# Sums of weights formed on GpSimd instead of VectorE in a Strassen-like feed-forward layer

## The chip, the cores and the metric

The kernel runs on one core of one Trainium2 chip. The metric is the device time of one execution in microseconds; the median over the timed runs is compared. The names of engines are those of the profile: PE is TensorE (its matmuls; PEld its weight loads), DVE is VectorE, ACT is ScalarE, POOL is GpSimd, and SP is SyncE, whose queue issues most DMAs.

## The reference, cut to what matters

One inference step of a small backbone: 2 layers, 640 tokens (512 latent and 128 context), model width 1024. Each layer is a half-step feed-forward, a token mixer (a two-dimensional Fourier transform in the first layer, attention in the second), and another half-step feed-forward, so there are four feed-forward stages in all. Each stage computes

```
def _swiglu(h, w1, w2):
    gate, up = jnp.split(h @ w1, 2, axis=-1)
    return (jax.nn.silu(gate) * up) @ w2
```

with a hidden width of 2816, which is 22 tiles of 128 ("f tiles"). Everything is float32. The other inputs are modulation weights (w_mod), which are multiplied with two condition vectors in the background of the other work.

## The kernel before, in words

**Precision.** Each product of float32 matrices is made as three matmuls of rounded parts (`mm3`, lines 228 to 230). For it every operand is split into a rounded part "hi", written by ACT (line 215), and the rest "lo" = operand - hi, written by DVE (line 216). Both the weights and the activations go through this split. Weight tiles are 128 x 1024 (a "unit"); they come by DMA into one of four buffers named raw, and the parts lie in six buffers each, named hi and lo. A unit is asked for three units ahead of its use in the code; the planner of the framework lays out the order on each engine from its own model of durations, so the splits run further ahead, as far as buffers allow.

**Seven products instead of eight.** The tokens are cut into two halves of 320. For the f tiles 4 to 21 (18 of 22 in each stage, 72 in all; `w1_fast`) the product of a 1024 x 256 piece of w1 (gate and up columns) with the two halves is made as a two-by-two block product in seven block products (Winograd's form of Strassen's method). Each block product is 4 x 3 = 12 matmuls of 128 x 320. To this end sums of the blocks are needed:

- Sums of activations, made once per stage (`combine`): b12 - b11 and so on, split into parts and kept in `sums[1]` to `sums[4]`.
- Sums of weights, made once per f tile (`send`, kinds "sums", "all" and "u2"). With `one` the first 512 columns of a raw tile and `two` the second 512: line 179 forms gate1 + up1, line 180 forms up1 + up2 in place, line 181 forms gate1 + (up1 + up2), and line 188 (for the last two f tiles of a stage line 197) forms the fourth one from the third and gate2. Each is one DVE instruction over 128 x 512.

In the code of one f tile (`w1_fast`, `one`, `two`) the order of products is: the first into bank x (kind main), the second into y (kind score), the third into z (main), the fourth into w (main), and then the fifth, sixth and seventh add to x, z and w. Between them small instructions on 128 x 320 read these banks: ACT copies x (line 687) before the fifth product may add to it; DVE forms q (690) from y, a (693) from z before the sixth may add to z, a again (713) from w before the seventh; the rest (698, 701, 702, 719 to 721) forms the hidden values, which are split again and kept for the second weight matrix. The main kind has four banks, the score kind two.

**Stages and slices.** After every fourth fast f tile a slice of the second matrix (w2) follows: 8 row tiles x 2 halves x 4 f tiles x 3 = 192 matmuls. Its results are added up by ACT, which puts the earlier sum into the bank before (line 737) and takes it out after (line 763). In the slices the background jobs run as well (line 421: one DMA of a raw tile of w_mod and two DVE instructions over 128 x 1024), 36, 12, 28, 32, 12 and 8 jobs in the six sub-layers.

**Order.** Each engine works through its own queue in order. A DVE instruction that stands behind a waiting one waits too, and so do those of ACT. POOL has hardly anything to do in the kernel before: a reciprocal root of three columns per normalisation (line 507), a few small differences and memsets in attention (lines 1041 and 1054), and two instructions in the last step (`leave`, lines 585 and 595).

Of the kernel before, what the change touches and what calls it, by code (L numbers as in the profile page):

```python
# [15 lines left out]
ALU = mybir.AluOpType  # L16
# [94 lines left out]
class Kernel:  # L111
# [54 lines left out]
    def send(self, kind, src):  # L166

        nc, two, one = self.nc, slice(512, UNIT), slice(0, 512)
        at = slice(0, UNIT)
        if kind in ("plain", "block", "gate"):
            raw = self.raw_tile(src)
            self.fast["gate"] = raw
        elif kind == "sums":
            up, gate = self.raw_tile(src), self.fast["gate"]
            raw = self.raw.tile([P, UNIT], F32, tag="raw", name=self.name("sums"))
            nc.vector.tensor_tensor(raw[:, one], gate[:, one], up[:, one], op=ALU.add)
            nc.vector.tensor_tensor(up[:, one], up[:, one], up[:, two], op=ALU.add)  # L180
            nc.vector.tensor_tensor(raw[:, two], gate[:, one], up[:, one], op=ALU.add)  # L181
            self.fast["up"], self.fast["sums"] = up, raw
        elif kind in ("up", "u2"):
            raw = self.fast["up"]
            at = at if kind == "up" else two
        else:
            raw, at = self.fast["gate"], two
            nc.vector.scalar_tensor_tensor(out=raw[:, two], in0=self.fast["sums"][:, two], scalar=-1.0,
                                           in1=raw[:, two], op0=ALU.mult, op1=ALU.subtract)
        n = at.stop - at.start  # L190
        if kind == "block":
            hi, lo = (self.ring(F32R)[:, :n] for _ in range(2))
        else:
            hi, lo = (self.wts.tile([P, UNIT], F32R, tag=tag, name=self.name(tag))[:, :n] for tag in ("hi", "lo"))
        self.split(hi, lo, raw[:, at])
        if kind == "u2":
            nc.vector.scalar_tensor_tensor(out=raw[:, two], in0=self.fast["sums"][:, two], scalar=-1.0,
                                           in1=self.fast["gate"][:, two], op0=ALU.mult, op1=ALU.subtract)
            self.mixed.append(raw)
        return hi, lo  # L200

# [400 lines left out]
    def ffn(self, layer, which, base, boundary):  # L602
# [43 lines left out]
        def combine(step):  # L646
# [10 lines left out]
            if step < 2:  # L657
                t = combine.now[k] = [self.temp(("square", "total")[step]).rearrange("p (c t) -> p c t", c=2)
                                      for _ in range(2)]
                steps = ((1, t[0], b12, b11), (2, t[1], b22, t[0]))  # L660
            else:
                t = combine.now[k]
                steps = ((3, t[0], b22, b12), (4, t[1], t[1], b21))
            for i, to, a, b in steps:
                if k == 0:
                    sums[i] = [quad(self.ring(F32R)) for _ in range(2)]
                nc.vector.tensor_tensor(to, a, b, op=ALU.subtract)
                self.split(sums[i][0][:, k : k + 2, :], sums[i][1][:, k : k + 2, :], to)

        high, tt = self.tc.high_priority, nc.vector.tensor_tensor  # L670
# [38 lines left out]
        def one(f, a, unit):  # L709
            w = self.bank()[:, :HALF]  # L710
            product(f, w, unit, 0, lambda k: part(1, k), True)
            with high():
                tt(a, a, w, op=ALU.add)
            return w

        def two(f, a, q, w, unit, at):
            product(f, w, unit, at, lambda k: self.h.chunk(4 + k, 1), False)
            with high():
                nc.vector.scalar_tensor_tensor(out=q, in0=w, scalar=-1.0, in1=q, op0=ALU.mult, op1=ALU.subtract)  # L719
                nc.scalar.activation(q, q, AF.Silu)  # L720
                tt(a, a, q, op=ALU.mult)
                hidden(f, a, 1)
# [708 lines left out]
```

## Time and profile before

| | |
|---|---|
| median of 3 runs | 2283.66 us |
| lowest and highest run | 2283.55 and 2283.94 us |
| span of the profiled execution (first to last instruction) | 2280.3 us |
| busy PE | 2250.1 us, 99% |
| busy DVE | 1732.2 us, 76% |
| busy ACT | 1269.6 us, 56% |
| busy POOL | 43.1 us, 2%, 64 instructions |
| mean granted clock of TensorE | 0.995 |

The time of the profiled execution outside its span isn't listed by itself; the median of the runs lies 3.4 us above the span. Busy times are shares of the span; matmuls overlap in the pipeline (one lasts about 310 ns but the next starts 147 ns after it), so a busy PE is to be checked against the distance of starts. In a row of a group stand the line, the engine, the operation, the tiles written and read with their shapes, the count, the busy time, the mean duration of one in ns, and the idle time of the engine ahead of it with what ended it.

### The profile page before, as it was taken

The page shows a single profiled execution, that of the slowest core. Times are in us where ns is not written, and L with a number is a line of the kernel's source. Part 1 is how long each engine was busy: PE and PEld are TensorE (multiplying, and loading weights), DVE is VectorE, ACT ScalarE, POOL GpSimd, SP SyncE. Part 2 cuts the span into 40 slices and gives each one's busy share as a digit, 9 for nine tenths or more (in the row PEclk, how much of TensorE's full clock was granted, in tenths as well). Part 3 has the DMA queues.
Part 4 walks back from the last instruction along what each step waited for, and adds up shares of the span by engine and source line. Part 5 has one row for each costly group of instructions (what it writes and reads, how often), then busy time and mean ns, then how long its engine had stood idle before and what let it go on. Part 6 is the DMA issues. An engine that isn't in the chain of part 4 may idle for free.

```text
span 2280.3 us, 39327 instructions
## 1 busy us (share of the span) xinstructions
PE 2250.1 (99%) x15680; PEld 2211.6 (97%) x15680; DVE 1732.2 (76%) x3014; ACT 1269.6 (56%) x2460; POOL 43.1 (2%) x64
## 2 busy tenths in 40 slices
PE   7999999999999999999999999999999999999998
PEld 5999999999999999999999999998998999999998
DVE  5889888588788888868878888587667485766674
ACT  4445554565654555556545544567778654545545
POOL 0000000000000000000000000000000000000000
PEclk9999999999999999999999999999999999999999
DMA  8244543434333433443234443324333223322322
GB/s 313 88 138 150 162 133 113 147 97 129 112 112 112 148 121 125 135 157 112 92 123 145 151 130 110 140 92 140 112 108 116 67 74 101 111 93 76 104 92 100
DMA packets 80281, 278.14 MB, mean 122 GB/s; under 512 B 8800, under 2 KB 15200, under 8 KB 79968
## 3 DMA queue, kind: packets, MB, share of 16 engines
q1 hardware_dynamic: 79280, 274.63, 36.4%
q8 instruction: 123, 2.02, 0.3%
q10 hardware_dynamic: 816, 0.98, 0.1%
q14 instruction: 62, 0.51, 0.1%
HBM read 264.04 MB, written 11.53 MB: 121 GB/s over the span
## 4 chain that ended last, share of the span: by engine, by line
PE 95%; DVE 2%; DMA 1%; ACT 1%; issue 0%; DVEq 0%; POOL 0%; SPq 0%
PE main L228 28%; PE main L230 27%; PE main L229 27%; PE score L229 3%; PE score L228 3%; PE score L230 3%; PE sum L1262 1%; PE score L1219 1%; PE sum L512 1%; PE sum L502 1%; DMA first<-in_w_mod_k 1%; PE turn L1246 1%; DVE lo L216 0%; PE main L1246 0%; DVE ring L1065 0%
## 5 line engine op out<-in xcount | busy, mean ns | idle before, releaser
L228 PE MATMUL main<-ring,hi 128*128 128x320 f32 x3872 | 1206.5, 312 | 2.0 <-ACT ring L215 1.6
L229 PE MATMUL main<-ring,hi 128*128 128x320 f32 x3872 | 1198.2, 310 | 1.0 <-DVE ring L216 1.0
L230 PE MATMUL main<-ring,lo 128*128 128x320 f32 x3872 | 1198.4, 310 | 0.0
L228 PEld LDWEIGHTS main<-ring,hi 128*128 128x128 f32 x3872 | 728.0, 188 | 8.4 <-issue 4.1
L229 PEld LDWEIGHTS main<-ring,hi 128*128 128x128 f32 x3872 | 728.3, 188 | 2.1 <-DVE ring L216 1.6
L230 PEld LDWEIGHTS main<-ring,lo 128*128 128x128 f32 x3872 | 728.0, 188 | 0.6 <-issue 0.5
L215 ACT ACTIVATE hi<-raw 128x1024 fp32r<-128x1024 f32 (+1 forms) x366 | 356.0, 974 | 433.7 <-PE main L229 349.2
L216 DVE TENSOR_TENSOR lo<-raw,hi 128x1024 fp32r<-128x1024 f32 (+1 forms) x366 | 409.0, 1118 | 140.8 <-ACT hi L215 139.4
L421 DVE SCALAR_TENSOR_TENSOR junk<-raw,wide 128x1024 bf16<-128x1024 f32 x256 | 312.7, 1222 | 19.7 <-DMA raw<-in_w_mod_t 17.2
L763 ACT ACTIVATE y<-main 128x320 f32<-128x320 f32 x318 | 135.7, 432 | 150.1 <-PE main L230 149.4
L737 ACT ACTIVATE main<-y 128x320 f32<-128x320 f32 x256 | 111.4, 439 | 39.2 <-DVE left L719 27.0
L228 PE MATMUL score<-ring,hi 128*128 128x320 f32 x416 | 128.9, 310 | 0.0
L230 PE MATMUL score<-ring,lo 128*128 128x320 f32 x416 | 128.6, 309 | 0.0
L229 PE MATMUL score<-ring,hi 128*128 128x320 f32 x416 | 128.5, 309 | 0.0
L216 DVE TENSOR_TENSOR lo<-sums,hi 128x1024 fp32r<-128x1024 f32 x72 | 88.0, 1222 | 42.6 <-ACT hi L215 42.6
L457 DVE TENSOR_TENSOR total<-total,square 128x640 f32<-128x640 f32 x71 | 58.4, 824 | 79.9 <-ACT square L456 78.2
L215 ACT ACTIVATE hi<-sums 128x1024 fp32r<-128x1024 f32 x72 | 76.3, 1060 | 33.8 <-DVE sums L181 19.6
L228 PE MATMUL main<-ring,ring 128*128 128x320 f32 x288 | 90.9, 316 | 0.0
L230 PE MATMUL main<-ring,ring 128*128 128x320 f32 x288 | 89.1, 310 | 0.0
L229 PE MATMUL main<-ring,ring 128*128 128x320 f32 x288 | 88.9, 309 | 0.0
L228 PEld LDWEIGHTS score<-ring,hi 128*128 128x128 f32 x416 | 78.1, 188 | 0.0
L229 PEld LDWEIGHTS score<-ring,hi 128*128 128x128 f32 x416 | 78.1, 188 | 0.0
(195 smaller groups left out, 2604.8 us busy)
## 6 DMA issues: line engine op xcount, KB each, us to landing
raw<-in_w SPq DMA_DIRECT2D x264, 512.0 KB, 3.6
raw<-in_w_mod_t SPq DMA_DIRECT2D x128, 512.0 KB, 4.1
raw<-in_qkv SPq DMA_DIRECT2D x26, 512.0 KB, 3.7
first<-in_w_mod_k SPq DMA_DIRECT2D x16, 512.0 KB, 8.9
spill<-ring SPq DMA_DIRECT2D x12, 640.0 KB, 3.8
ring<-spill SPq DMA_DIRECT2D x12, 640.0 KB, 7.0
raw<-in_bias SPq DMA_DIRECT2D x16, 448.0 KB, 3.4
raw<-in_four_in SPq DMA_DIRECT2D x8, 512.0 KB, 5.7
```

What stands on the lines that cost most here:

```text
L215: a = self.nc.scalar.activation(hi, src, AF.Copy)
L216: return a, self.nc.vector.tensor_tensor(lo, src, hi.bitcast(F32), op=ALU.subtract)
L228: mm(out, whi, xhi, start=start, stop=False)
L229: mm(out, whi, xlo, start=False, stop=False)
L230: self.latest = mm(out, wlo, xhi, start=False, stop=stop)
L421: last = self.nc.vector.scalar_tensor_tensor(out=self.junk, in0=raw, scalar=1.0, in1=self.wide[:, cond, :], op0=ALU.mult, op1=ALU.mult, ac ...
L457: nc.vector.tensor_tensor(acc, acc, sq, op=ALU.add)
L502: self.meant = nc.tensor.matmul(ps[:, j : j + 1], part[:, t : t + P], self.mean, start=i == j == 0 or len(acc) == 1, stop=i == len(acc) - ...
L512: self.spread = nc.tensor.matmul(bank[:, t : t + P], col[:, j : j + 1].to_broadcast([P, P]), self.ident, start=True, stop=True)
L737: nc.scalar.activation(ps[:, :HALF], self.y[:, m, lo:hi], AF.Copy)
L763: nc.scalar.activation(self.y[:, m, lo:hi], ps[:, :HALF], AF.Copy)
L1219: nc.tensor.matmul(o, q, k[:, BLOCK_KEYS[b]], start=part == 0, stop=part == 1)
```

## The change

The three sums of kind "sums" and the fourth one of kinds "all" and "u2" go from `nc.vector` to `nc.gpsimd`. The fourth was formed as (-1) x sums - gate2 in one instruction of the kind scalar_tensor_tensor. On GpSimd it is a plain add, sums + gate2, which is the negative of what it was. To keep the result, the activation sum that meets w's products is formed with the opposite sign as well (b11 - b12 instead of b12 - b11, and the next sum adds it instead of subtracting it), so that bank w holds the negative of what it held, and the two DVE instructions that read w (lines 713 and 719 before) subtract in place of adding, and w - q in place of -w - q. The count of instructions is the same: 288 move from DVE to POOL (72 at each of lines 179 to 181, 64 at line 188, 8 at line 197).

```
         elif kind == "sums":
             up, gate = self.raw_tile(src), self.fast["gate"]
             raw = self.raw.tile([P, UNIT], F32, tag="raw", name=self.name("sums"))
-            nc.vector.tensor_tensor(raw[:, one], gate[:, one], up[:, one], op=ALU.add)
-            nc.vector.tensor_tensor(up[:, one], up[:, one], up[:, two], op=ALU.add)
-            nc.vector.tensor_tensor(raw[:, two], gate[:, one], up[:, one], op=ALU.add)
+            nc.gpsimd.tensor_tensor(raw[:, one], gate[:, one], up[:, one], op=ALU.add)
+            nc.gpsimd.tensor_tensor(up[:, one], up[:, one], up[:, two], op=ALU.add)
+            nc.gpsimd.tensor_tensor(raw[:, two], gate[:, one], up[:, one], op=ALU.add)
             self.fast["up"], self.fast["sums"] = up, raw
...
-            nc.vector.scalar_tensor_tensor(out=raw[:, two], in0=self.fast["sums"][:, two], scalar=-1.0,
-                                           in1=raw[:, two], op0=ALU.mult, op1=ALU.subtract)
+            nc.gpsimd.tensor_tensor(raw[:, two], self.fast["sums"][:, two], raw[:, two], op=ALU.add)
...
         if kind == "u2":
-            nc.vector.scalar_tensor_tensor(out=raw[:, two], in0=self.fast["sums"][:, two], scalar=-1.0,
-                                           in1=self.fast["gate"][:, two], op0=ALU.mult, op1=ALU.subtract)
+            nc.gpsimd.tensor_tensor(raw[:, two], self.fast["sums"][:, two], self.fast["gate"][:, two], op=ALU.add)
...
-                steps = ((1, t[0], b12, b11), (2, t[1], b22, t[0]))
+                steps = ((1, t[0], b11, b12, ALU.subtract), (2, t[1], b22, t[0], ALU.add))
...
-                steps = ((3, t[0], b22, b12), (4, t[1], t[1], b21))
-            for i, to, a, b in steps:
+                steps = ((3, t[0], b22, b12, ALU.subtract), (4, t[1], t[1], b21, ALU.subtract))
+            for i, to, a, b, op in steps:
...
-                nc.vector.tensor_tensor(to, a, b, op=ALU.subtract)
+                nc.vector.tensor_tensor(to, a, b, op=op)
...
             with high():
-                tt(a, a, w, op=ALU.add)
+                tt(a, a, w, op=ALU.subtract)
...
-                nc.vector.scalar_tensor_tensor(out=q, in0=w, scalar=-1.0, in1=q, op0=ALU.mult, op1=ALU.subtract)
+                tt(q, w, q, op=ALU.subtract)
```

## The prediction

> **What bounds the kernel now.** I read the page first (busy shares, the strip of slices, the chain that ended last), then busy time by stretch.
>
> ```profile
> span 2280.3 us, 39327 instructions
> PE 2250.1 (99%) x15680; PEld 2211.6 (97%) x15680; DVE 1732.2 (76%) x3014; ACT 1269.6 (56%) x2460; POOL 43.1 (2%) x64
> ...
> PE 95%; DVE 2%; DMA 1%; ACT 1%; issue 0%; DVEq 0%; POOL 0%; SPq 0%
> ```
>
> TensorE holds 95% of the chain. A busy PE need not be at its peak, so I check the rate in a stretch that the change touches. One f tile with seven products runs 7 x 12 matmuls; its second product goes to a bank named score, so the first score matmul marks the tile. The next two fences are the timeline of TensorE, and then the busy time of one whole cycle (four fast f tiles and one slice of the second weight matrix, 77.44 us) in each of the four feed-forward stages.
>
> ```profile
> 212.37 0.31 PE L228 MATMUL score<-ring,hi 128*128 128x320 f32 x1
> ...
> 302.12 0.31 PE L228 MATMUL score<-ring,hi 128*128 128x320 f32 x1
> ...
> 314.44 0.31 PE L228 MATMUL score<-ring,hi 128*128 128x320 f32 x1
> ```
>
> ```profile
> 133.17:210.61 77.44, 77.44 (x531) 77.44 (x530) 68.29 (x111) 40.53 (x72) 0.00 (x0) 1.00 0.44 142
> 717.56:795.00 77.44, 77.44 (x530) 77.44 (x529) 63.96 (x104) 40.71 (x72) 0.00 (x0) 1.00 0.40 130
> 1158.22:1235.66 77.44, 77.44 (x530) 77.44 (x529) 65.85 (x106) 40.59 (x72) 0.00 (x0) 1.00 0.42 136
> 1929.59:2007.03 77.44, 77.44 (x530) 77.44 (x529) 51.95 (x80) 40.85 (x72) 0.00 (x0) 1.00 0.30 96
> ```
>
> After the stretch and its length the columns are the busy time of PE, PEld, DVE, ACT, POOL, then clock and DMA. Tile follows tile after 314.44 - 302.12 = 12.32 us, which is 84 matmuls at 0.1467 us; 528 matmuls (4 x 84 and 192 for the slice) at 0.1467 are 77.45 us, the whole cycle. So PE has no hole in these cycles, at full clock. A product of 12 matmuls is 1.76 us. DVE is the second engine: 68.29 of 77.44 (88%) in the first stage, 83%, 85% and 67% in the others.
>
> **What the change can win at most.** Where sums are formed outside these cycles, PE is short of the stretch by this much:
>
> ```profile
> 399.00:684.00 285.00, 284.89 (x1989) 280.12 (x1988) 219.83 (x366) 165.72 (x319) 9.63 (x8) 1.00 0.35 119
> 969.00:1117.00 148.00, 147.01 (x1006) 145.64 (x1005) 110.89 (x169) 89.74 (x167) 3.78 (x4) 1.00 0.34 119
> 1482.00:1824.00 342.00, 335.70 (x2569) 314.87 (x2567) 240.55 (x614) 250.46 (x622) 18.49 (x37) 0.99 0.34 106
> ```
>
> That is 0.11 and 0.99 us at the two crossings between stages; the 6.30 us of the third stretch lie in attention, which forms no sums. So the relief of DVE is worth at most about 1 us directly.
>
> **Removed from DVE.** The rows by line and form:
>
> ```profile
> L181 DVE TENSOR_TENSOR sums<-raw,raw 128x512 f32<-128x512 f32 x72 | 49.7, 691 | 1.9
> L180 DVE TENSOR_TENSOR raw<-raw 128x512 f32<-128x512 f32 x72 | 49.7, 690 | 1.7
> L179 DVE TENSOR_TENSOR sums<-raw,raw 128x512 f32<-128x512 f32 x72 | 49.4, 686 | 16.3 <-DMA raw<-in_w 15.7 <-DVE left L713 0.4
> L188 DVE SCALAR_TENSOR_TENSOR raw<-sums,raw 128x512 f32<-128x512 f32 x64 | 44.1, 689 | 0.9
> L197 DVE SCALAR_TENSOR_TENSOR raw<-sums,raw 128x512 f32<-128x512 f32 x8 | 5.5, 689 | 0.1
> ```
>
> 49.7 + 49.7 + 49.4 + 44.1 + 5.5 = 198.4 us in 288 instructions of 0.69 us, sixteen per cycle: 11.0 us. All of it is off the path, since PE is full beside it. The exchanged signs at L667, L713 and L719 keep one DVE instruction each: nothing. No DMA and no product is added or moved on SP.
>
> **Added on POOL.** No POOL row has 128x512. The nearest rows are a smaller and a larger one:
>
> ```profile
> L1054 POOL TENSOR_TENSOR ring<-ring,ring x16: 452/457/1367, 1532.2 to 1726.2; 64x128 fp32r<-64x128 f32 x16
> ```
>
> ```profile
> L585 POOL TENSOR_TENSOR y<-y,rms 128x640 f32<-128x640 f32 x1 | 1.5, 1544 | 2.2 <-ACT rms L579 2.2
> ...
> L595 POOL TENSOR_TENSOR ring<-ring,y 128x640 f32<-128x640 f32 x1 | 2.0, 1992 | 0.1
> ```
>
> The shortest with 128 elements took 452 ns and the free one with 640 took 1544 ns, 2.13 ns per element between them, so 512 elements come to 452 + 384 x 2.13 = 1271 ns. Bounds are 452 and 1544; I take 1.27, which lies on the line between. 288 x 1.27 = 366 us of POOL, 16 x 1.27 = 20.3 per cycle: POOL is a quarter full and no bound by itself.
>
> **What an add on POOL costs DVE.** Here the last few us of the kernel are the evidence, where both engines do the same work side by side:
>
> ```profile
> 2271.27 2.28 DVE L585 TENSOR_TENSOR y<-y,sum 128x640 f32<-128x640 f32 x3 [1.96 <-PE sum L512]
> 2273.47 3.28 DVE L595 TENSOR_TENSOR ring<-ring,y 128x640 f32<-128x640 f32 x2
> ...
> 2272.45 1.54 POOL L585 TENSOR_TENSOR y<-y,rms 128x640 f32<-128x640 f32 x1 [2.21 <-ACT rms L579]
> 2274.07 1.99 POOL L595 TENSOR_TENSOR ring<-ring,y 128x640 f32<-128x640 f32 x1
> ...
> L595 DVE TENSOR_TENSOR ring<-ring,y x2: 1207/1677/2147, 2273.5 to 2274.6; 128x640 f32<-128x640 f32 x2
> ...
> L562 DVE TENSOR_TENSOR y<-y,rms 128x640 f32<-128x640 f32 x44 | 34.7, 820 | 9.6 <-ACT rms L518 9.6
> ```
>
> The three DVE instructions at L585 read PSUM (sum) and one SBUF tile and were not stretched (2.28 us for three) though POOL worked from 2272.45 on. The two at L595 read two SBUF tiles and took 1207 and 2147 ns where 820 is usual, and POOL's own second one took 1992 instead of 1544. They went by turns: POOL to 2273.99, DVE, POOL to 2276.06, DVE. So a DVE instruction with two SBUF inputs and a POOL add wait for each other. The longer wait, 2147 - 820 = 1327 ns for 640 elements, scales to 1.06 us for 512. Bounds per add: nothing (POOL hits an idle DVE or one that reads PSUM) and 1.27 (the whole add). I take 1.06, because most DVE time is of the two-SBUF kind, above all the splits and the products of w_mod:
>
> ```profile
> L216 DVE TENSOR_TENSOR lo<-raw,hi 128x1024 fp32r<-128x1024 f32 x294 | 359.5, 1223 | 119.3 <-ACT hi L215 118.1
> L421 DVE SCALAR_TENSOR_TENSOR junk<-raw,wide 128x1024 bf16<-128x1024 f32 x256 | 312.7, 1222 | 19.7 <-DMA raw<-in_w_mod_t 17.2
> ```
>
> [...]
>
> DVE per cycle, before - 11.0 + 16 x 1.06 (in brackets with 1.27), of 77.44: first stage 68.29 - 11.0 + 17.0 = 74.3 (77.6); second 70.0 (73.3); third 71.9 (75.2); fourth 58.0 (61.3). At the price I take every cycle still fits.
>
> **Lag within a cycle.** The heaviest part is the slice and the tile behind it in the first stage, and what PE can tolerate is read from DVE's timeline behind it:
>
> ```profile
> 182.45:210.61 28.16, 28.16 (x195) 28.16 (x194) 27.47 (x47) 16.45 (x35) 0.00 (x0) 1.00 0.52 168
> 210.61:222.93 12.32, 12.32 (x87) 12.32 (x86) 10.18 (x16) 5.35 (x8) 0.00 (x0) 1.00 0.31 96
> ```
>
> ```profile
> 210.22 0.69 DVE L179 TENSOR_TENSOR sums<-raw,raw 128x512 f32<-128x512 f32 x1
> 210.95 0.69 DVE L180 TENSOR_TENSOR raw<-raw 128x512 f32<-128x512 f32 x1
> 211.67 0.69 DVE L181 TENSOR_TENSOR sums<-raw,raw 128x512 f32<-128x512 f32 x1
> ...
> 213.49 1.23 DVE L216 TENSOR_TENSOR lo<-sums,hi 128x1024 fp32r<-128x1024 f32 x1 [0.40 <-ACT hi L215]
> ...
> 216.09 0.49 DVE L693 TENSOR_TENSOR left<-left,main 128x320 f32<-128x320 f32 x1 [0.96 <-PE main L230]
> ```
>
> Four sums fall into the slice: 27.47 - 2.8 + 4.2 = 28.9 for 28.16, a lag of 0.7. Six start in the tile: 10.18 - 4.1 + 6.4 = 12.5 for 12.32: lag 0.9. With 1.27 it is 1.6 and 3.3. What DVE must not be late for: L693 reads the bank of the third product before the sixth adds to it, which starts 4 x 1.76 after the score row, 219.41. L693 ended 216.58, 2.83 us early, and had waited 0.96 for PE before. So a lag of 0.9 costs nothing, and one of 3.3 nothing or little.
>
> **The sums' own latency.** Three adds took 210.22 to 212.36 = 2.14 us; on POOL 3 x 1.27 = 3.8, and up to 7.5 if each waits for a DVE instruction of 1.22 first. POOL is not queued behind DVE's order, so it can start at the landing. Behind the wait for the sums stands ACT's split, and behind that in ACT's order the copy that frees the first product's bank:
>
> ```profile
> 212.40 1.06 ACT L215 ACTIVATE hi<-sums 128x1024 fp32r<-128x1024 f32 x1 [1.10 <-DVE sums L181]
> 213.37 0.41 ACT L687 ACTIVATE left<-main 128x320 f32<-128x320 f32 x1
> ```
>
> L687 must end before the fifth product, 212.37 + 3 x 1.76 = 217.65; it ended 213.78, 3.87 early. The split weights (ready at 214.72) are for the next tile's second product, 212.37 + 12.32 = 224.69: 10.0 us early. An extra 1.7 us passes under both. L188's add moves out of DVE's queue, so the sums buffer comes free no later.
>
> **The sum.** 0 gained in the cycles, at most 1 at the crossings, and I allow 1 to 2 us for tiles in the first stage where DVE was already behind: against this execution 2280.3 + 1.3 = 2281.6 of span. The median of the runs lies 3.4 above the span, so the forecast is 2285; its own range is 2282 to 2288.
>
> **Rivals.**
> 1. Slower: DVE becomes the bound through the shared access. For it: the L595 rows, and 96 to 100% by the sums above. Against it: 2.83 us of tolerance, and cover from PSUM readers. Were half of DVE's idle time not usable (waits for PE or ACT: 4.6, 6.7, 5.8, 12.7 per cycle), the excess per cycle at 1.06 would be 1.5, 0, 0.3, 0 and at 1.27 4.8, 2.6, 3.6, 0; times four cycles per stage 7 to 44 us, in the middle 25: 2309. It decides from 0.97 us per add in the first stage (57.3 + 16b + 4.6 = 77.44), 1.05 in the third, 1.12 in the second.
> 2. Slower: ACT stands in its queue at the split of the sums. At 7.5 us instead of 2.14 it is 5.4 late, 1.5 beyond L687's 3.87; once for each of the 16 cycles 24 us, by half 12: 2296. It needs three full waits in a row, and an early start of POOL works against it.
> 3. Faster: the planner orders other work anew, and two thirds of the 7.4 us of PE holes shown above go: 2278.7. Nothing in the profile asks for that.
>
> **How the numbers follow.** Forecast 0.50, rival 1 0.25, rival 2 0.15, rival 3 0.10. A measurement of this kernel tells a difference from about 0.2%, 4.6 us. So faster 0.10, same 0.50, slower 0.40. The range is 2278 (rival 3) to 2309: it holds the price of rival 2 and the lower half of rival 1, and leaves out the upper half of rival 1 (some 0.12) and a little below.
>
> **What would show it.** Right: L179 to L181 on POOL near 1.27 us plus waits, POOL busy near 410, score to score 12.32 everywhere, PE equal to the stretch in the four cycles. The exclusion shows as L216 and L421 above 1222 ns and DVE busy above 1732 - 198 = 1534 by up to 366. Rival 1: DVE near 77 of the cycle, and L228 of the sixth or seventh product waiting for L693 or L713. Rival 2: ACT's wait for the sums far above its present 19.6 us in the row below, with PE waiting for L687.
>
> ```profile
> ACT hi L215 <- DVE sums L181: 19.6, 17, 3.4
> ```
>
> The forecast is wrong if an add takes well over 1.54 us, or if most adds hold DVE for their whole length.

## The result, and the profile after

The changed kernel takes 2347.77 us (median of 4 runs, 2347.16 to 2350.31) against 2283.61 us for the kernel before on the same chip: a ratio of 1.0288, 95% interval 1.0276 to 1.0300. It is 64 us slower, and the prediction (2285, at most 2309) was wrong. The span of the profiled execution is 2348.5 - 2280.3 = 68.2 us longer. The differences by stretch below are of the profiled executions and add up to this, not to the 64 us of the medians; counted from the first matmul, as there, it is 68.6 us.

The page of the changed kernel, first its span, the busy time of each engine and the chain that ended last:

```profile
span 2348.5 us, 39658 instructions
PE 2274.9 (97%) x15680; PEld 2228.5 (95%) x15680; DVE 1682.7 (72%) x2726; ACT 1259.3 (54%) x2460; POOL 471.9 (20%) x352
...
PE 73%; DVE 9%; DMA 6%; POOL 5%; ACT 4%; issue 4%; DVEq 0%; POOLq 0%; SPq 0%; ACTq 0%
```

DVE lies 49.5 us below its 1732.2 of before, and its share fell from 76% to 72%. The engine that was relieved is relieved. The chain, though, was PE by 95% and is so by 73% now; DVE, DMA, POOL and ACT stand in it with 24% together. That is the picture of a chain of hand-overs on which PE waits, and not of a full engine. The groups by line and form (busy time, mean ns of one, idle time ahead and what ended it; in this kernel the lines below the sums are two less than before, so the splits are L213 on ACT and L214 on DVE):

```profile
L214 DVE TENSOR_TENSOR lo<-raw,hi 128x1024 fp32r<-128x1024 f32 x294 | 373.7, 1272 | 109.2 <-ACT hi L213 107.7
L419 DVE SCALAR_TENSOR_TENSOR junk<-raw,wide 128x1024 bf16<-128x1024 f32 x256 | 331.3, 1294 | 31.4 <-DMA raw<-in_w_mod_t 27.8
...
L180 POOL TENSOR_TENSOR raw<-raw 128x512 f32<-128x512 f32 x72 | 112.2, 1558 | 5.7
L179 POOL TENSOR_TENSOR sums<-raw,raw 128x512 f32<-128x512 f32 x72 | 112.1, 1558 | 836.0 <-DVE junk L419 250.2 <-DMA raw<-in_w 244.5 <-DVE lo L214 113.4
L181 POOL TENSOR_TENSOR sums<-raw,raw 128x512 f32<-128x512 f32 x72 | 109.8, 1525 | 5.6
L188 POOL TENSOR_TENSOR raw<-sums,raw 128x512 f32<-128x512 f32 x64 | 83.9, 1311 | 164.1 <-DVE lo L214 136.6 <-issue 25.2
```

The three adds of a chain take 1558 + 1558 + 1525 = 4.64 us on the mean, 2.5 us more than the 2.14 us on DVE. And these are the waits that answer to the row which the prediction named (us in total, times, longest):

```profile
ACT hi L213 <- POOL sums L181: 136.3, 40, 6.1
...
PE main L226 <- ACT main L735: 17.4, 15, 1.9
...
PE main L226 <- DVE left L691: 13.2, 7, 3.2
```

ACT waits for the sums 136.3 us in place of 19.6. PE waits for what ACT and DVE do behind that.

**Where the loss lies.** A stretch is compared from one matmul to the same matmul of the other kernel. For the second stage: the cycles with slices, and then its late tiles, which are the last two fast f tiles with the work around them. Busy time by stretch, the kernel before:

```profile
717.56:975.11 257.55, 257.55 (x1759) 257.55 (x1757) 210.68 (x340) 133.90 (x234) 0.00 (x0) 1.00 0.39 124
975.11:1026.01 50.90, 50.86 (x347) 50.59 (x346) 29.17 (x44) 28.22 (x51) 0.00 (x0) 1.00 0.47 171
```

and the changed kernel:

```profile
739.20:1000.47 261.27, 258.33 (x1758) 257.54 (x1757) 200.49 (x284) 130.62 (x233) 83.37 (x56) 1.00 0.39 122
1000.47:1059.37 58.90, 54.14 (x348) 53.07 (x346) 27.41 (x39) 29.31 (x52) 6.87 (x5) 0.94 0.42 151
```

The cycles lose 3.7 us of 258 and the late tiles 8.0 of 51. The same subtraction for every stage and kernel, in us over the kernel before (worked out from the starts of the same matmuls in the profiled executions, counted from the first matmul; "first tiles" is the way to the first cycle of the first stage). Each row is one execution: that of e10 was the shortest of its four runs (2320.46 us, median 2323.76), that of e12 the longest (2327.73, median 2322.10).

| kernel | first tiles | cycles, stages 1 / 2 / 3 / 4 | late tiles, 1 / 2 / 3 / 4 | rest | sum |
|---|---|---|---|---|---|
| changed kernel | 8.7 | 5.8 / 3.7 / 5.0 / 7.9 | 7.1 / 8.0 / 8.0 / 6.8 | 7.6 | 68.6 |
| e11_third_pool | 0.3 | 0 / 0 / 0 / 0 | 0.8 / 0.2 / 0 / 0 | -0.5 | 0.8 |
| e14_two_pool | 1.8 | 3.8 / 0 / 0.4 / 0 | 0.9 / 1.5 / 0.9 / 0.9 | 0.8 | 11.0 |
| e3_three_pool | 5.2 | 7.0 / 3.1 / 3.9 / 9.4 | 3.1 / 2.6 / 1.6 / 1.5 | 6.5 | 43.9 |
| e2_fourth_pool | -0.6 | 0.1 / 0 / 0 / 0 | 1.2 / 1.0 / 0.5 / 0.6 | -1.0 | 1.8 |
| e6_dose | 9.3 | 23.0 / 10.5 / 12.8 / 11.0 | 10.5 / 10.6 / 9.5 / 8.5 | 13.6 | 119.3 |
| e5_idle_adds | 2.0 | 17.5 / 0.2 / 6.2 / 0.3 | 2.3 / 3.5 / 2.2 / 0.9 | 9.8 | 44.9 |
| e1_hold | 5.2 | 18.5 / 6.8 / 4.3 / 1.2 | 3.7 / 4.1 / 5.0 / 3.5 | 5.1 | 57.4 |
| e7_hold_both | 3.5 | 7.5 / 0.9 / 0.9 / 0 | 5.8 / 3.4 / 4.8 / 3.2 | 5.0 | 35.0 |
| e13_hold_half_gemv | 4.3 | 6.2 / 3.6 / 0.6 / 0 | 6.3 / 3.5 / 3.7 / 3.6 | 5.3 | 37.1 |
| e9_five_raw_before | -1.0 | 0 / 0 / 0 / 0 | 0 / -0.3 / 0 / 0 | 5.4 | 4.1 |
| e10_five_raw_after | 5.5 | 2.9 / 5.4 / 3.7 / 0 | 0.6 / 0.3 / 0.6 / 0.6 | 18.9 | 38.5 |
| e12_hold_and_raw | 12.1 | 8.0 / 0 / 0.6 / 0 | 1.1 / 4.5 / 1.0 / 1.5 | 16.7 | 45.5 |

In the changed kernel 22.4 us lie in the cycles and 29.9 in the late tiles, though only 8 of the 72 f tiles are late ones. In its cycles PE stands idle for 4.3, 2.9, 4.1 and 5.6 us in the four stages, in 14 waits, and every one of them ends with a seed (L735, ACT puts the earlier sum into a bank of the slice). In 12 of the 14, three in each stage, that seed stands in ACT's queue behind the split of the sums, for which ACT had waited 4.1 to 5.1 us; the other two are of 0.34 and 0.19 us. What remains of the 22.4 us, 5.5, was not split further.

**A stall in a cycle.** One of these waits is shown here: the timeline of the changed kernel in the fourth stage (start, duration, instruction; in brackets the idle time ahead of it and what ended it), with the matmul that PE issued late:

```profile
2033.28 2.02 POOL L179 TENSOR_TENSOR sums<-raw,raw 128x512 f32<-128x512 f32 x1 [22.55 <-DMA raw<-in_w]
...
2035.38 1.43 POOL L180 TENSOR_TENSOR raw<-raw 128x512 f32<-128x512 f32 x1
2036.88 1.28 POOL L181 TENSOR_TENSOR sums<-raw,raw 128x512 f32<-128x512 f32 x1
2038.20 1.06 ACT L213 ACTIVATE hi<-sums 128x1024 fp32r<-128x1024 f32 x1 [4.68 <-POOL sums L181]
...
2039.16 0.42 ACT L735 ACTIVATE main<-y 128x320 f32<-128x320 f32 x1
...
2039.64 0.42 PE L226 MATMUL main<-ring,hi 128*128 128x320 f32 x1 [1.80 <-ACT main L735]
```

POOL starts at the landing, as predicted. The first add is stretched to 2.02 us, all three are done after 4.88 us, and ACT has stood idle for 4.68 us at the split. The seed of a bank of the slice (L735, 0.42 us of work, with no wait of its own in the trace) stands behind the split in ACT's queue, and PE waits 1.80 us for it.

**The loop of the late tiles.** There the changed kernel shows:

```profile
1006.72 1.30 POOL L196 TENSOR_TENSOR raw<-sums,raw 128x512 f32<-128x512 f32 x1 [6.70 <-DVE lo L214]
...
1011.78 1.43 POOL L179 TENSOR_TENSOR sums<-raw,raw 128x512 f32<-128x512 f32 x1 [3.77 <-DMA raw<-in_w]
...
1014.78 1.30 POOL L181 TENSOR_TENSOR sums<-raw,raw 128x512 f32<-128x512 f32 x1
1016.11 1.06 ACT L213 ACTIVATE hi<-sums 128x1024 fp32r<-128x1024 f32 x1 [3.55 <-POOL sums L181]
...
1017.21 1.23 DVE L214 TENSOR_TENSOR lo<-sums,hi 128x1024 fp32r<-128x1024 f32 x1 [3.65 <-ACT hi L213]
...
1019.58 1.42 POOL L196 TENSOR_TENSOR raw<-sums,raw 128x512 f32<-128x512 f32 x1 [3.50 <-DVE lo L214]
...
1021.03 12.83 SPq L157 DMA_DIRECT2D raw<-in_w  x5
1025.32 1.06 ACT L213 ACTIVATE hi<-raw 128x1024 fp32r<-128x1024 f32 x1 [4.39 <-DMA raw<-in_w]
...
1031.19 1.06 ACT L213 ACTIVATE hi<-raw 128x1024 fp32r<-128x1024 f32 x1 [0.43 <-DMA raw<-in_w]
...
1032.28 1.23 DVE L214 TENSOR_TENSOR lo<-raw,hi 128x1024 fp32r<-128x1024 f32 x1 [1.27 <-ACT hi L213]
...
1033.42 0.48 DVE L691 TENSOR_TENSOR left<-left,main 128x320 f32<-128x320 f32 x1
...
1033.96 0.64 PE L226 MATMUL main<-ring,hi 128*128 128x320 f32 x1 [3.08 <-DVE left L691]
```

and the kernel before, in the same tile:

```profile
981.25 0.69 DVE L197 SCALAR_TENSOR_TENSOR raw<-sums,raw 128x512 f32<-128x512 f32 x1
982.00 27.82 SPq L157 DMA_DIRECT2D raw<-in_w  x7
...
986.01 0.69 DVE L179 TENSOR_TENSOR sums<-raw,raw 128x512 f32<-128x512 f32 x1
...
988.41 0.68 DVE L181 TENSOR_TENSOR sums<-raw,raw 128x512 f32<-128x512 f32 x1
...
993.22 0.69 DVE L197 SCALAR_TENSOR_TENSOR raw<-sums,raw 128x512 f32<-128x512 f32 x1
```

The next load of a raw tile is issued at 1021.03, the first of the five in its row, as the fourth sum ends (1019.58 + 1.42 = 1021.00): the add gives a raw buffer back. Before it was the same (981.25 + 0.69 = 981.94, and 982.00). The load lands 4 us later, and only then come adds, splits and the next fourth sum. In these tiles the raw buffers are the loop: from fourth sum to fourth sum it took 993.22 - 981.25 = 11.97 us before, less than the 12.32 us of a tile, and takes 1019.58 - 1006.72 = 12.86 us now (11.97 in all four stages before, 12.78 to 12.88 now). In the steady tiles the split weights are 10 us early; here that margin isn't renewed, and PE runs into holes, the largest of this stage 3.08 us behind a subtraction (L691 at 1033.42) that stood in DVE's queue behind the lo half of a late load (1032.28).

### The profile page after: what moved, and what is told of

The parts are those of the page before. It is cut to its first block, busy times and chain, and to the rows that moved or that the text cites. A ratio compares the mean times of both kernels' runs of the same rounds, so it can differ in the third digit from the quotient of the medians.

```text
span 2348.5 us, 39658 instructions
## 1 busy us (share of the span) xinstructions
PE 2274.9 (97%) x15680; PEld 2228.5 (95%) x15680; DVE 1682.7 (72%) x2726; ACT 1259.3 (54%) x2460; POOL 471.9 (20%) x352
## 3 DMA queue, kind: packets, MB, share of 16 engines
q8 instruction: 123, 2.02, 0.4%
## 4 chain that ended last, share of the span: by engine, by line
PE 73%; DVE 9%; DMA 6%; POOL 5%; ACT 4%; issue 4%; DVEq 0%; POOLq 0%; SPq 0%; ACTq 0%
PE main L226 21%; PE main L227 20%; PE main L228 20%; DVE lo L214 3%; DMA raw<-in_w 3%; DMA raw<-in_w_mod_t 2%; ACT hi L213 2%; PE score L227 2%; PE score L226 2%; PE score L228 2%; POOL sums L179 2%; POOL raw L180 2%; DVE junk L419 2%; POOL sums L181 1%; PE sum L1260 1%
## 5 line engine op out<-in xcount | busy, mean ns | idle before, releaser
L226 PE MATMUL main<-ring,hi 128*128 128x320 f32 x3872 | 1216.3, 315 | 43.9 <-ACT main L735 17.4
L214 DVE TENSOR_TENSOR lo<-raw,hi 128x1024 fp32r<-128x1024 f32 (+1 forms) x366 | 448.8, 1228 | 173.8 <-ACT hi L213 172.3
L213 ACT ACTIVATE hi<-raw 128x1024 fp32r<-128x1024 f32 (+1 forms) x366 | 355.9, 973 | 391.7 <-PE main L227 275.0
L419 DVE SCALAR_TENSOR_TENSOR junk<-raw,wide 128x1024 bf16<-128x1024 f32 x256 | 331.3, 1294 | 31.4 <-DMA raw<-in_w_mod_t 27.8
L179 POOL TENSOR_TENSOR sums<-raw,raw 128x512 f32<-128x512 f32 x72 | 112.1, 1558 | 836.0 <-DVE junk L419 250.2
L214 DVE TENSOR_TENSOR lo<-sums,hi 128x1024 fp32r<-128x1024 f32 x72 | 93.8, 1302 | 132.6 <-ACT hi L213 132.6
L761 ACT ACTIVATE y<-main 128x320 f32<-128x320 f32 x318 | 133.6, 429 | 101.7 <-PE main L228 100.8
L213 ACT ACTIVATE hi<-sums 128x1024 fp32r<-128x1024 f32 x72 | 76.0, 1056 | 143.8 <-POOL sums L181 136.3
L505 POOL TENSOR_TENSOR col<-col,power 128x3 f32<-128x3 f32 x24 | 26.4, 1099 | 623.1 <-DVE col L504 623.1
L735 ACT ACTIVATE main<-y 128x320 f32<-128x320 f32 x256 | 111.4, 439 | 48.9 <-DVE left L717 23.2
L188 POOL TENSOR_TENSOR raw<-sums,raw 128x512 f32<-128x512 f32 x64 | 83.9, 1311 | 164.1 <-DVE lo L214 136.6
L180 POOL TENSOR_TENSOR raw<-raw 128x512 f32<-128x512 f32 x72 | 112.2, 1558 | 5.7
L181 POOL TENSOR_TENSOR sums<-raw,raw 128x512 f32<-128x512 f32 x72 | 109.8, 1525 | 5.6
```

The lines of the kernel that those rows point to most:

```text
L179: nc.gpsimd.tensor_tensor(raw[:, one], gate[:, one], up[:, one], op=ALU.add)
L180: nc.gpsimd.tensor_tensor(up[:, one], up[:, one], up[:, two], op=ALU.add)
L181: nc.gpsimd.tensor_tensor(raw[:, two], gate[:, one], up[:, one], op=ALU.add)
L188: nc.gpsimd.tensor_tensor(raw[:, two], self.fast["sums"][:, two], raw[:, two], op=ALU.add)
L213: a = self.nc.scalar.activation(hi, src, AF.Copy)
L214: return a, self.nc.vector.tensor_tensor(lo, src, hi.bitcast(F32), op=ALU.subtract)
```

## Experiments

All changes are to the changed kernel unless another is named. The expectations call A the theory that the order of a queue (a split waiting for its sums with urgent work behind it) makes the loss, and B that it is the time which each add takes from DVE; a further letter is explained where it stands.

**How many adds, and where.** Five kernels differ only in which sums POOL forms. The fourth sum alone:

```
-            nc.gpsimd.tensor_tensor(raw[:, one], gate[:, one], up[:, one], op=ALU.add)
+            nc.vector.tensor_tensor(raw[:, one], gate[:, one], up[:, one], op=ALU.add)
-            nc.gpsimd.tensor_tensor(up[:, one], up[:, one], up[:, two], op=ALU.add)
+            nc.vector.tensor_tensor(up[:, one], up[:, one], up[:, two], op=ALU.add)
-            nc.gpsimd.tensor_tensor(raw[:, two], gate[:, one], up[:, one], op=ALU.add)
+            nc.vector.tensor_tensor(raw[:, two], gate[:, one], up[:, one], op=ALU.add)
```

> Only the fourth sum of each f tile is on POOL, the first three are on DVE. Theory A: ACT's split of the three sums waits for DVE as before, so within 6 us of 2283.6. Theory B: a quarter of the adds, a quarter of the loss: 2300 us. Theory C: sums and gate buffers are released as before or earlier, within 6 us.

Measured 2286.29 us, ratio 1.0015 (1.0005 to 1.0024), as A and C had it and not B. The three of the chain, with the fourth on DVE:

```
-            nc.gpsimd.tensor_tensor(raw[:, two], self.fast["sums"][:, two], raw[:, two], op=ALU.add)
+            nc.vector.tensor_tensor(raw[:, two], self.fast["sums"][:, two], raw[:, two], op=ALU.add)
...
-            nc.gpsimd.tensor_tensor(raw[:, two], self.fast["sums"][:, two], self.fast["gate"][:, two], op=ALU.add)
+            nc.vector.tensor_tensor(raw[:, two], self.fast["sums"][:, two], self.fast["gate"][:, two], op=ALU.add)
```

> The first three sums are on POOL, the fourth is on DVE. Theory A: the whole loss stays, 2338 to 2352 us. Theory B: three quarters of the loss, 2332 us. Theory C: most of the loss, 2335 to 2350 us.

Measured 2324.61 us, 1.0175 (1.0157 to 1.0193): 42 us, less than each of the three theories had said. The third alone (L179, L180, L188 and L196 on DVE):

```
-            nc.gpsimd.tensor_tensor(raw[:, one], gate[:, one], up[:, one], op=ALU.add)
+            nc.vector.tensor_tensor(raw[:, one], gate[:, one], up[:, one], op=ALU.add)
-            nc.gpsimd.tensor_tensor(up[:, one], up[:, one], up[:, two], op=ALU.add)
+            nc.vector.tensor_tensor(up[:, one], up[:, one], up[:, two], op=ALU.add)
             nc.gpsimd.tensor_tensor(raw[:, two], gate[:, one], up[:, one], op=ALU.add)
...
-            nc.gpsimd.tensor_tensor(raw[:, two], self.fast["sums"][:, two], raw[:, two], op=ALU.add)
+            nc.vector.tensor_tensor(raw[:, two], self.fast["sums"][:, two], raw[:, two], op=ALU.add)
...
-            nc.gpsimd.tensor_tensor(raw[:, two], self.fast["sums"][:, two], self.fast["gate"][:, two], op=ALU.add)
+            nc.vector.tensor_tensor(raw[:, two], self.fast["sums"][:, two], self.fast["gate"][:, two], op=ALU.add)
```

> Only the third of the three sums (the last of the chain that ACT's split waits for) is on POOL; the other three are on DVE. One add in the chain, a quarter of the adds. Theory A and C with slack in the chain: the split is only 0.6 us later than before, within 8 us of the kernel before. If every add in the chain costs the same, a third of the 42 us that three adds cost: 2297 us. Theory B: a quarter of 64, 2299 us.

Measured 2282.99 us beside 2282.71, 1.0002 (0.9993 to 1.0012). The second and third (L179, L188, L196 on DVE):

```
-            nc.gpsimd.tensor_tensor(raw[:, one], gate[:, one], up[:, one], op=ALU.add)
+            nc.vector.tensor_tensor(raw[:, one], gate[:, one], up[:, one], op=ALU.add)
             nc.gpsimd.tensor_tensor(up[:, one], up[:, one], up[:, two], op=ALU.add)
             nc.gpsimd.tensor_tensor(raw[:, two], gate[:, one], up[:, one], op=ALU.add)
...
-            nc.gpsimd.tensor_tensor(raw[:, two], self.fast["sums"][:, two], raw[:, two], op=ALU.add)
+            nc.vector.tensor_tensor(raw[:, two], self.fast["sums"][:, two], raw[:, two], op=ALU.add)
...
-            nc.gpsimd.tensor_tensor(raw[:, two], self.fast["sums"][:, two], self.fast["gate"][:, two], op=ALU.add)
+            nc.vector.tensor_tensor(raw[:, two], self.fast["sums"][:, two], self.fast["gate"][:, two], op=ALU.add)
```

> The first and the fourth sum of weights stay on DVE, the second and the third are formed by POOL: two adds of the chain, where the third sum alone measured 2283.0 (no loss) and all three 2324.6 (42 us). Theory A (the chain of the sums has some slack, and what it is late beyond that is paid by PE): the second add still lies partly within the slack, so less than half of the 42 us: 2284 to 2303. Theory B (each add costs the same, by what it takes from DVE): two thirds of 42 us, 28 us: 2307 to 2315. If it is all a step (a full chain on POOL is needed), no loss: 2282 to 2285.

Measured 2293.45 us, 1.0048 (1.0032 to 1.0065): 11 us. And the first add of the changed kernel made twice, the second time with the same result:

```
             nc.gpsimd.tensor_tensor(raw[:, one], gate[:, one], up[:, one], op=ALU.add)
+            nc.gpsimd.tensor_tensor(raw[:, one], gate[:, one], up[:, one], op=ALU.add)
```

> The changed kernel with the first sum formed twice in a row on POOL (one more add of about 1.5 us in the chain of each f tile). Theory A: PE stalled once in each of 16 cycles and in the last two tiles of four stages, 24 places at 1.5 us, 36 us more: 2378 to 2390 us. Theory B: a fourth more adds, a fourth more loss, 16 us more: 2364 us. Theory C: as theory A or less, 2365 to 2385 us.

Measured 2403.98 us, 1.0535 (1.0518 to 1.0551): 121 us, 57 more than the changed kernel. With none of the adds moved, one, two and three of the chain, the loss is 0, 0, 11 and 42 us; with the fourth sum 64, with one add more in the chain 121. The last is more than any theory had said. In the chain each add costs more than the one before (0, 11 and 31 us, and 57 for the one made twice). A fixed price per add, which is how B was put, would give a straight line, so B in that form falls. A chain with some slack fits: the first add hides in it, and from the second on PE pays. A DVE that gets too full would bend the line too; the runs below bear on that. Also, e2 and e11 carry the exchanged signs, and e11 loses nothing: the signs are free, as forecast. The fourth sum costs 3.6 us by itself, but 22 us (64 - 42) behind three slow ones; 21.1 of the 24.7 us between e3 and the changed kernel in the table lie in the late tiles, whose loop it closes.

**Adds that nobody waits for.** To the kernel *before*, five adds of 128x384 per f tile on POOL whose result isn't read:

```
             self.fast["up"], self.fast["sums"] = up, raw
+            for _ in range(5):
+                nc.gpsimd.tensor_tensor(self.spare, gate[:, :384], gate[:, :384], op=ALU.add)
```

The tile that they write takes the place of one that was set once and never read (`ones`); the trace shows nobody who waits for these adds.

> The kernel before (sums on DVE), with five further POOL adds of 128x384 per f tile that read the gate tile and write a tile that nobody reads: 360 adds at about 1.0 us, 360 us of POOL work that reads SBUF, as much as in the change, with nobody waiting for it. ACT's order is that of the kernel before. Theory A: within 5 us of 2283.6. Theory B: at least 2320 us, since the shared access is loaded as in the change while DVE also keeps its own sums. Theory C: within 5 us.

Measured 2327.93 us, 1.0200 (1.0185 to 1.0216): 45 us, as B had said; A and C, with at most 5 us, were off. Its busy times, and the row of the adds:

```profile
PE 2265.9 (97%) x15680; PEld 2216.3 (95%) x15680; DVE 1868.0 (80%) x3013; ACT 1258.5 (54%) x2460; POOL 462.6 (20%) x424
...
L184 POOL TENSOR_TENSOR spare<-raw 128x384 bf16<-128x384 f32 x360 | 419.5, 1165 | 1011.6 <-DMA raw<-in_w 988.5
```

DVE grows by 1868.0 - 1732.2 = 135.8 us, 0.38 per add. So POOL's adds do lengthen DVE's work: the split (L218 of this kernel, 128x1024) takes 1327 ns where it took 1223, the last product of an f tile (L722, no operand in PSUM) 693 where it took 485, and L694, which reads a bank in PSUM, 486 where it took 487. Where DVE keeps its own sums as well, that costs: 17.5 of the 45 us lie in the cycles of the first stage and 6.2 in those of the third, the two with the fullest DVE, and next to nothing in the second and fourth. This is the loss that rival 1 described. The changed kernel doesn't show its pattern: there the fourth stage, with DVE emptiest, loses most in its cycles (7.9 us), and PE waits for seeds, whereas here its waits in the first stage's cycles end almost all (10.5 of 10.7 us) with the copies and subtractions of an f tile (L688 and L694 of this kernel).

**The order of the queues.** The split of the sums on ACT is put behind the newest copy of a bank (L685) or eviction (L761) in the order of its queue:

```
-        self.split(hi, lo, raw[:, at])
+        with self.behind_of(*self.evicted) if kind == "sums" else ExitStack():
+            self.split(hi, lo, raw[:, at])
...
+                self.evicted = (nc.scalar.activation(a, x, AF.Copy),)
...
+                self.evicted = (nc.scalar.activation(self.y[:, m, lo:hi], ps[:, :HALF], AF.Copy),)
```

> The four sums stay on POOL as in the changed kernel; only ACT's split of the three sums is ordered behind the newest copy that takes a bank out (the copy of the first product in an f tile, or the copy of a slice's result). Theory A (ACT stands in its queue at the split of the sums, and the copies behind it keep PE's banks): PE's waits for ACT's seeds and copies go, at least 45 of the 64 us come back, 2283 to 2303 us. Theory B (DVE and POOL keep each other from SBUF): nothing changes on that, 2335 to 2350 us. Theory C (the raw buffers are held longer, so loads come late): the split comes later still, 2345 us or more.

Measured 2337.79 us, 1.0248 (1.0229 to 1.0268): only 10 us back, less than A had said (2283 to 2303) and within what B had said (2335 to 2350). The timeline of this kernel in the first stage shows that this needn't mean B:

```profile
310.62 1.06 ACT L215 ACTIVATE hi<-sums 128x1024 fp32r<-128x1024 f32 x1 [5.45 <-POOL sums L182]
...
311.72 1.32 DVE L216 TENSOR_TENSOR lo<-sums,hi 128x1024 fp32r<-128x1024 f32 x1 [3.65 <-ACT hi L215]
...
313.55 0.49 DVE L693 TENSOR_TENSOR left<-left,main 128x320 f32<-128x320 f32 x1
...
314.09 0.41 PE L228 MATMUL main<-ring,hi 128*128 128x320 f32 x1 [2.35 <-DVE left L693]
```

Now it is DVE that stands for 3.65 us at the lo half of the same split, with the subtraction of z (L693) behind it, for which PE waits 2.35 us. The queue of one engine was cured, and the wait went to the other one. So both halves are held, the DVE subtraction (L691 in the changed kernel) being added to what the split stands behind:

```
-                tt(a, q, z, op=ALU.subtract)
+                self.evicted += (tt(a, q, z, op=ALU.subtract),)
```

> As e1_hold, and DVE's half of the split of the three sums is held back too, behind the subtraction that reads the third product's bank (L693 before). In e1_hold DVE stood at this split for 3.6 us with L690 and L693 behind it. Theory A, widened (each in-order queue that carries the split, ACT's and DVE's, makes the copies and subtractions behind it late): most of what e1_hold left comes back except in the last f tiles of a stage, 2300 to 2318 us. Theory B (DVE and POOL exclude each other): 2330 us or more. Theory C (raw buffers are held longer and loads come late): 2335 us or more.

Measured 2316.79 us, 1.0151 (1.0136 to 1.0166): 31 us of the 64 are back. Its second stage, cycles and late tiles:

```profile
736.12:994.56 258.44, 258.31 (x1756) 257.64 (x1757) 207.43 (x287) 131.20 (x235) 90.51 (x58) 1.00 0.40 127
994.56:1048.86 54.30, 52.38 (x347) 52.12 (x346) 30.34 (x39) 28.58 (x52) 9.86 (x7) 0.97 0.44 157
```

The cycles lose 0.9, 0.9 and 0 us in the second to fourth stage where the changed kernel loses 3.7, 5.0 and 7.9, with the same adds on POOL. That shows that late sums cost PE there by way of the two queues. Their order is not the only cure: with a fifth raw buffer and no hold (e10 below) the cycles of the fourth stage lose nothing either. The first stage (7.5) doesn't come back, and of the late tiles 17.2 of 29.9 us stay. In the first stage the trace shows the queue again, one instruction further on: all of PE's idle time in these cycles, 4.6 us in 5 waits, ends with the next subtraction (L713 of this kernel), which stands behind the held lo half. In one of them DVE waited 2.65 us before that half (at 306.04) and PE then 1.42 us for L713.

To see whether DVE's load holds the rest of the first stage, half of the background work is left out in addition (the products of w_mod with the second condition vector, so the outputs that depend on it are not computed):

```
-                        self.gemv(self.raw_tile(self.io["w_mod_t"][layer, j]), layer, j)
+                        self.gemv(self.raw_tile(self.io["w_mod_t"][layer, j]), layer, j, (0,))
```

> e7_hold_both with half of the background products on DVE left out (the second condition's, 128 instructions of 1.2 us; its modulation values are then missing, the rest is computed). e7_hold_both still lost 7.5 us over the kernel before in the cycles of the first feed-forward stage, where DVE is fullest, and 0 to 0.9 in the other three. Theory B for this remainder (DVE, held up by POOL's reads, is full there): it falls under 2 us, and the whole to 2303 to 2311 us. If it is the queues or the raw buffers still, it stays at 5 us or more: 2312 us or more.

Measured 2318.55 us, 1.0156 (1.0141 to 1.0171), no better than e7. Fewer DVE instructions don't shorten what is left, against B's forecast.

**One raw buffer more.** For room the ring of activation blocks gives one up:

```
-NRAW = 4
-NBLK = 20
+NRAW = 5
+NBLK = 19
```

First in the kernel *before*, to know the price of the room:

> The kernel before with five raw buffers and 19 block buffers instead of four and 20, as the partner of the next run. All theories: 2275 to 2295 us.

Measured 2287.70 us, 1.0021 (1.0012 to 1.0031). Then in the changed kernel:

> The changed kernel with five raw buffers and 19 block buffers. Theory C (the longer adds hold one of four raw buffers at a time, so the next loads and the next adds start late): the distance to its partner shrinks from 64 to at most 25 us, the last f tiles of each stage (some 28 us of the loss) recover first. Theory A alone: the adds are as long, the split stands at the same place in the queue, distance 45 us or more. Theory B: distance 50 us or more.

Measured 2323.76 us, 1.0191 (1.0169 to 1.0213). The change of engine costs 2323.76 - 2287.70 = 36 us with five raw buffers and 64 with four. The late tiles of the second stage here:

```profile
997.99:1049.16 51.17, 50.86 (x347) 50.59 (x346) 27.95 (x39) 28.10 (x51) 7.47 (x5) 1.00 0.45 166
```

51.17 us where the changed kernel takes 58.90 and the kernel before 50.90; in all four stages the late tiles go from 29.9 us of loss to 2.1. From fourth sum to fourth sum it is 10.18 us here. So the shortage of raw buffers is what these tiles lose by. The queues have a part in it, since the holds of e7 take 12.7 of the 29.9 us away with four buffers. The 36 us lie between what C had said (at most 25) and A (45 or more): outside of cycles and late tiles this kernel loses more than the changed one (rest 18.9 for 7.6).

**Both cures.** The two holds of e7 and five raw buffers together:

> The held-back splits of e7_hold_both and the five raw buffers (19 block buffers) of e10_five_raw_after together. If the two causes are separate (A: the queues lose in the cycles; C: the raw buffers lose in the last f tiles of a stage), the gains add up: last f tiles +1 us or less per stage over the kernel before, cycles as in e7_hold_both or less, 2296 to 2308 us in all. If they are one and the same cause, no better than the better of the two: 2314 to 2324 us.

Measured 2322.10 us, 1.0172 (1.0153 to 1.0191): no better than either, which is the time that was forecast for one and the same cause; the forecast for two separate ones (2296 to 2308) failed. By the table the cycles of the later stages are cured (0, 0.6 and 0) and the late tiles mostly (8.1 together, 2.1 in e10), but 12.1 us are lost in the first tiles, 8.0 in the cycles of the first stage, and 16.7 in the rest, where the fifth buffer alone loses 5.4 (e9). In the first stage's cycles PE's idle time, 4.7 us in 3 waits, ends with a seed (L737 of this kernel) again; before the longest ACT stood 5.52 us at a split for a load (DMA), not for the sums. What delays that load, and what the other places lose by, wasn't settled, so that the two parts add up is not shown.

No kernel that was run is faster than the kernel before.

## Why the prediction was wrong, point by point

- **PE is full, nothing to win.** Right. e11, which takes 72 instructions from DVE at no cost elsewhere, gains nothing (2282.99 beside 2282.71).
- **198.4 us leave DVE, and part comes back beside POOL's adds.** Right in kind, the size was taken too high. Of 1732.2 - 198.4 = 1533.8 us the busy time rose to 1682.7, so 148.9 us came back, 0.52 us per add, half of the 1.06 taken. The rows named for it rose too: the split from 1223 to 1272 ns, the products of w_mod from 1222 to 1294. The lo half of the hidden values, which wasn't named, rose most, from 485 to 819 ns (104 times), and a row that reads a bank in PSUM not at all (L693, now L691: 487 both times), as the prediction had it. Single pairs stretch by more (a POOL add of 2.02 us, in e1 a product of w_mod of 2.33 where 1.22 is usual), but the 0.52 us over the mean of all adds is less than half of an add of 1.31 to 1.56 us.
- **Rival 1, DVE as the bound.** Didn't decide. In the changed kernel's cycles of the second stage DVE is busy 200.49 of 261.27 us, 77%, less than before (210.68 of 257.55, 82%); e13, with less for DVE, is no faster; e5 shows what it looks like where it does decide. (In the working before it, the lag of the slice and its tile at 1.27 us per add comes to 27.47 - 2.8 + 5.1 - 28.16 = 1.6 and 1.6 + 10.18 - 4.1 + 7.6 - 12.32 = 3.0, not 3.3; nothing hangs on it.)
- **A POOL add takes 1.27 us.** Right for one outside the three in a row (L188: 1311 ns on the mean, the shortest 1266), too low on the mean for the three in a row (1558, 1558, 1525).
- **The step that failed** is the one on the sums' own latency: "An extra 1.7 us passes under both". It has three faults. The extra is 2.5 us on the mean, and 4.88 - 2.14 = 2.7 in the stall shown. The margin of 3.87 us was read from one tile behind a slice, and taken for all: it isn't there in the slices, where the seeds (L735) stand behind the split, nor in DVE's queue behind the lo half, which the prediction didn't examine at all. And the loop by the raw buffers wasn't examined: the prediction said that with L188's add out of DVE's queue "the sums buffer comes free no later", but in the late tiles the fourth sum ends later, the next load is issued at its end, and the loop of 11.97 us, 0.35 us below the tile's 12.32, became one of 12.86. In these tiles lie 29.9 us, the largest part, and with a fifth raw buffer 27.8 of them are gone. The length of the loop alone doesn't give the size: in e3, with the fourth sum on DVE, it is 12.80 to 12.97 us and the late tiles lose 8.8. There DVE's queue has the subtraction ahead of the late lo half in the place of the 3.08 us (L691 at 1024.35, L214 at 1025.29), and PE waits 0.31 us.
- **Rival 2, ACT stands at the split of the sums.** The mechanism is right: ACT's wait went from 19.6 to 136.3 us, and PE waits for what stands behind it. In the cycles this is the seeds; the copy that the prediction named (L687, now L685) ends a wait of PE in the late tiles only, 4.9 us in four, behind the same split. Its price of 12 to 24 us is of the size of the 22.4 us that the cycles lost, but it was counted for cycles only, and nothing was counted for the late tiles, the first tiles (8.7) and the rest (7.6). That alone put the time outside the range. Two waits outside of cycles and late tiles are the same thing with another instruction: 1.47 us at 124.90 and 1.94 us at 1181.32 end with an eviction (L761) behind a split of the sums for which ACT had waited 5.66 and 6.12 us.
- **Rival 3, faster by a new order.** Nothing of it. The crossings that were short by 0.11 and 0.99 us got longer (by 0.4 and 7.2 us, in the "rest" of the table).

Open are most of the first tiles and of the rest (the largest other holes of PE there, 2.70 us at 70.28 and 2.14 us at 1115.79, end with L636 and L491 on DVE), the cycles of the first stage after both cures, and what the changed order of the planner adds to each part; a kernel with the old order written out by hand and POOL's adds in it wasn't tried.

## What to carry to other kernels

Work that lies in a chain (load, sums, split, product) isn't sped up by a lower busy share of an engine: what counts here is how much longer the chain gets, and how much slack it has at its tightest place. Look for that place behind each waiting instruction in *both* queues that it passes, and in the loop that gives its buffers back; read it at the ends of a stage too, not in the steady part alone. The relief of an engine that wasn't the bound was worth nothing here (e11), so the move had only a price.

## What the runs showed of the hardware that was not expected

**A hole in PE cost more than its length.** Around the hole of 3.08 us in the late tiles of the second stage the changed kernel shows, in stretches of 4 us (the column before the last two is the granted clock):

```profile
1028.47:1032.47 4.00, 1.97 (x12) 1.48 (x10) 2.19 (x5) 2.44 (x5) 0.00 (x0) 1.00 0.83 242
1032.47:1036.47 4.00, 2.51 (x9) 2.52 (x10) 1.43 (x2) 0.54 (x2) 0.00 (x0) 0.51 0.47 151
1036.47:1040.47 4.00, 4.00 (x20) 4.00 (x20) 1.81 (x4) 2.23 (x4) 0.00 (x0) 0.64 0.00 1
```

and over the whole execution:

```profile
core 0: 2348.5 us, clock 0.988
```

In the stretch with the rest of the hole the granted clock is 0.51, in the next one 0.64, and there 20 matmuls take 4.00 us instead of 20 x 0.1467 = 2.9. From 1033.96 to 1039.2, some 5 us, matmuls start 0.267 us apart on the mean, behind that 0.147 again. The mean clock of the execution fell from 0.995 to 0.988; (1 - 0.988) x 2348.5 - (1 - 0.995) x 2280.3 = 16.8 us, at most about a quarter of the loss, went to the clock and not to the waits themselves. This is an estimate from the means, and high, since the clock is already low in a part of the holes (0.54 from 1032.50 to 1033.00 and 0.50 from there to 1033.50, with PE idle). In the stretch of the late tiles above PE's busy time rose by 54.14 - 50.86 = 3.3 us of the 8.0, at a granted clock of 0.94; with five raw buffers it is 50.86 again at 1.00. The hole shown is 3.08 us long (half of it lies in the first stretch, where PE is busy for 1.97 of 4.00 us). One of 1.92 us at 2198.82 was followed by a clock of 0.63 over 4 us, and one of 2.46 us at 439.52 by 1.00 over 4 us, so the length of the hole alone doesn't decide. The last two stretches shown hold 9 + 20 matmuls, which want 29 x 0.1467 = 4.3 us, in 8 us with PE idle for 1.5 of them: 2.2 us went to the clock. So this stall of 3.1 us cost 5.3.

**POOL adds stretch where DVE's work stands in line.** The same add takes 1311 ns at L188 and 1558 at L179 and L180, a fifth more, and in single cases up to 2.3 us, though DVE is busy for 72% only. In one chain that meets two products of w_mod the two engines go by turns: POOL's three adds start at 1173.10, 1174.52 and 1176.75 and take 1.34, 2.15 and 2.15 us, DVE's products start at 1173.19 and 1175.57 and take 2.33 and 2.19 us, where 1.30 and 1.22 are usual. Why the adds behind a landing meet DVE more often than the fourth sum was not tried.
